# Low parts of 17 projection weights: a subtraction on VectorE replaced by a negated copy on ScalarE and an adding transfer

## The chip, the cores and the metric

The kernel runs on one core of one Trainium2 chip. The metric is the device time of one execution in microseconds; the median of three runs is compared. A core has a matrix engine (TensorE, PE in the profile, with its weight loads as PEld), three engines for elementwise work (VectorE or DVE, ScalarE or ACT, GpSimd or POOL), and SyncE (SP), which here only issues transfers. All engines run their own instruction queues in order and wait for each other through semaphores. Transfers run on 16 DMA engines beside them.

## The reference

One layer of a diffusion backbone on 512 latent tokens and 256 context tokens, width 1024, all in float32. Cut to what matters here:

```
mod = silu(c) @ w_mod + b_mod                        # shift, scale, gate
h   = rms_norm(x) * (1 + scale) + shift              # 512 + 256 tokens
cq, ckv, kr, z, xbc, dt = split(h @ w_in, [384, 256, 32, 1024, 1536, 32])
q   = rms_norm(cq) @ w_q_up ;  k, v = rms_norm(ckv) @ w_kv_up
attn = softmax(q k^T) v                              # 16 heads
ssd  = chunked bidirectional scan(silu(conv(xbc)), dt) * silu(z), normalised
x   = x + gate * rms_norm([attn, ssd] @ w_out)
x   = x + gate2 * rms_norm((gelu(conv(h2 @ w_gate)) * (h2 @ w_val)) @ w_down)
```

The columns of `w_in` for `xbc` (12 blocks of 128), `cq` (3 blocks) and `ckv` (2 blocks) are the weights in question.

## The kernel before

TensorE is used in its fast float32r format, which rounds its operands. To keep the precision, an operand `x` is split into a high part `hi = round(x)` and a low part `lo = x - hi`, both in float32r, and each product is made three times: hi·hi, hi·lo, lo·hi. `split` (line 504) does this: ScalarE copies (line 506), VectorE or, where a caller says so, GpSimd subtracts (line 507). `weight` (line 509) gets a tile, loads 128 rows of a weight through SP (`load`, line 497), gets two more tiles for the parts, and splits.

The input projection is worked in blocks of 128 output columns. `xbc(m)` (line 780, m from 0 to 11) takes one 128x1024 weight, multiplies it with the modulated tokens (`gemm_T`, line 756: 8 row blocks times 3 products, for the 512 latent tokens and, below m = 10, for the 256 context tokens), and runs the convolution on ScalarE (line 787) and VectorE (line 791). `latent` (line 822) does the same for the low-rank queries and keys/values, with sums of squares on GpSimd (line 840). Called first are xbc(10), xbc(11) and `latent("wcq")` (lines 869 to 871), then xbc(8, 0, 1, 2, 3) (line 891); the rest of the input projection (line 972) runs beside the state scan `ssd` (line 991), whose products with the decay are on GpSimd (lines 1024, 1033). Before all this TensorE works on the z projection (`half_of_z`, line 691; its product is line 693), and parts of the second half of z are spread among the later work.

The order on every engine is not that of the text. The program is traced once, then `plan` (line 389) computes a list schedule of all instructions from a table of costs, assigns buffers (53 blocks of 1024 columns, cut into 212 units), repeats this 24 times, and keeps the order with the smallest sum; in the second tracing that order is written down for every engine. So any change of an instruction or of a cost gives a new order and new buffers for the whole kernel. In that schedule a transfer is booked with an issue time (`issue`, line 200), a start latency (`DMA_START`, line 147), its bytes at 360 GB/s (`price`, line 157) and a wait (`DMA_WAIT`); for one issued by an engine other than SP (lines 357 to 360), the issuing engine was booked for 60 ns. Before the change GpSimd issues no transfer; SP issues nearly all and ScalarE a few.

Attention, the output projection (line 1318) and the MLP (line 1445 and behind) follow; they use `weight` and `split` unchanged.

Of the kernel before, what the change touches and what calls it, by code (L numbers as in the profile page):

```python
# [13 lines left out]
AF = mybir.ActivationFunctionType  # L14
ALU = mybir.AluOpType
# [131 lines left out]
DMA_START, DMA_WAIT, DMA_AHEAD, DMA_ALONE, RUN, FLYING, DMA_FULL, DMA_FILLS = 650, 910, 3000, 0.8, 80, 8, 600, 40000  # L147
# [116 lines left out]
class Graph:  # L264
# [48 lines left out]
    def schedule(self, rank, look=0.06):  # L313

        n = len(self.preds)
        left, ready = [len(p) for p in self.preds], [0.0] * n
        start, end = [0.0] * n, [0.0] * n
        later, now = {e: [] for e in ENGINES}, {e: [] for e in ENGINES}
        clock, order, queue = {e: 0.0 if self.back else BEGIN for e in ENGINES}, {e: [] for e in ENGINES}, 0.0
        ticks, held, port, flying = {}, 0, 0.0, []  # L320
        for i in range(n):
            if not left[i]:
                ready[i] = max(0.0, rank[i] - AHEAD) if i in self.opens else 0.0
                heapq.heappush(later[self.eng[i]], (ready[i], rank[i], i))

        def open_until(e, t):
            while later[e] and later[e][0][0] <= t:
                _, r, i = heapq.heappop(later[e])
                heapq.heappush(now[e], (r, i))

        for _ in range(n):
            while True:
                at = []
                for e in ENGINES:
                    open_until(e, clock[e])
                    if now[e] or later[e]:
                        at.append((clock[e] if now[e] else later[e][0][0], e))
                t, e = min(at, key=lambda v: v[0])
                open_until(e, t)
                r, i = heapq.heappop(now[e])  # L340
                sooner = [v for v in later[e] if v[1] < r and v[0] < t + (look if v[1] > r - 5000 else 0.8) * self.cost[i]]
                if not sooner:
                    break
                heapq.heappush(now[e], (r, i))
                clock[e] = min(sooner, key=lambda v: v[1])[0]
            order[e].append(i)
            if self.tables[i] not in (None, held):
                held, t = self.tables[i], t + TABLE
            if self.shared[i]:
                t = max(t, port)  # L350
                port = t + self.cost[i]
            if self.dma[i] and not self.back and len(flying) >= FLYING:
                t = max(t, flying[-FLYING])
            start[i] = t
            end[i] = t + self.cost[i] if self.back or e != "PE" else self.product(t, i, ticks)
            clock[e] = end[i] + (3 if e == "PE" else 0)
            if self.dma[i] and e != "SP":
                began = t + self.dma[i] + DMA_START + 600
                queue = max(began, queue) + self.cost[i]
                end[i], clock[e] = queue + DMA_ALONE * self.cost[i], t + 60  # L360
            if e == "SP":
                began = t + self.dma[i] + DMA_START
                queue = max(began, queue) + self.cost[i]
                end[i] = queue + DMA_ALONE * self.cost[i]
                if not self.back and t < DMA_FILLS:
                    end[i] = max(began + (1 + DMA_ALONE) * self.cost[i], queue - DMA_FULL)
                clock[e] = t + self.dma[i] if self.back else max(t + self.dma[i], queue - DMA_AHEAD)
            if self.dma[i]:
                flying.append(end[i] + DMA_WAIT)
            for j in self.succs[i]:  # L370
                ready[j] = max(ready[j], end[i] + self.wait(i, j))
                left[j] -= 1
                if not left[j]:
                    if j in self.opens:
                        ready[j] = max(ready[j], rank[j] - AHEAD)
                    heapq.heappush(later[self.eng[j]], (ready[j], rank[j], j))
        return max(end), order, start, end
# [97 lines left out]
def build(nc, tc, ctx, a, out, dbg=None, places=None):  # L475
    mm = nc.tensor.matmul
    act = nc.scalar.activation
    V, G = nc.vector, nc.gpsimd
# [10 lines left out]
    def t4(*shape, dt=F32):  # L489
        return sl.get(here(), shape or (P, 1024), dt)  # L490

    def t2(*shape, dt=F32):
        return sl.get(here(), shape or (P, 512), dt)
# [3 lines left out]
    def load(dst, src, q=None):  # L497
        (q or nc.sync).dma_start(out=dst, in_=src)
# [5 lines left out]
    def split(hi, lo, src, lo_eng=None):  # L504

        act(hi, src, AF.Copy)  # L506
        (lo_eng or V).tensor_tensor(out=lo, in0=src, in1=hi, op=ALU.subtract)  # L507

    def weight(src, width=1024, lo_eng=None):

        tw = t2 if width <= 512 else t4
        raw = tw(P, width)
        load(raw, src)
        w = tw(P, width, dt=F32R), tw(P, width, dt=F32R)
        split(*w, raw, lo_eng)
        return w

    smalls = c_([P, 512], "smalls")
# [237 lines left out]
    def gemm_T(wf, nk, cols, parts=((0, 0), (0, 1), (1, 0))):  # L756

        for k in range(nk):
            for pt in parts:
                for po, xf in cols:  # L760
                    mm(po, lhsT=wf(k, pt[0]), rhs=xf(k, pt[1]), start=(k == 0 and pt == parts[0]),  # L761
                       stop=(k == nk - 1 and pt == parts[-1]))
# [15 lines left out]
    xs, bn, bct = [None] * 2, [None] * 2, [None] * 2  # L778

    def xbc(m):  # L780
        w = weight(a["wxbc"][m])
        g = (m % 8) // 4 if m < 8 else m % 2
        pm = pget("a")
        gemm_T(blk(w), KD, both(pm) if m < 10 else ((pm[:, :S], hxv),))
        st = t4(P, T)
        for o, n in ((0, S), (S, CT))[: 2 if m < 10 else 1]:
            act(st[:, o : o + n], pm[:, o : o + n], AF.Identity, scale=cwh[:, m * 5 + 2 : m * 5 + 3], bias=cbh[:, m : m + 1])  # L787
            for j in (0, 1, 3, 4):
                d = j - 2
                lo, hi = o + max(0, -d), o + n - max(0, d)  # L790
                V.scalar_tensor_tensor(out=st[:, lo:hi], in0=pm[:, lo + d : hi + d], scalar=cwh[:, m * 5 + j : m * 5 + j + 1],  # L791
                                       in1=st[:, lo:hi], op0=ALU.mult, op1=ALU.add)
        pfree(pm)

        th = t4(P, T)
        n = T if m < 10 else S
        act(th[:, :n], st[:, :n], AF.Tanh)
        if m >= 10:
            bct[g] = t4(P, 2, S)
            V.scalar_tensor_tensor(out=bct[g][:, 1, :], in0=th[:, :S], scalar=1.0, in1=st[:, :S], op0=ALU.add, op1=ALU.mult)  # L800
            return
        V.scalar_tensor_tensor(out=st, in0=th, scalar=1.0, in1=st, op0=ALU.add, op1=ALU.mult)
        tx, tc_ = pget("b"), pget("b")
        for c in range(NKT):
            o = (c if c < NX else c - NX) * P
            nc.tensor.transpose((tx if c < NX else tc_)[:, o : o + P], st[:, c * P : (c + 1) * P], ident)
        if m < 8:
            if m % 4 == 0:
                xs[g] = [t4(P, 2, 512) for _ in range(3)]
            o = (m % 4) * P  # L810
            for i in range(3):
                src = tx[:, i * 256 : i * 256 + 256] if i < 2 else tc_[:, :256]
                act(xs[g][i][:, :, o : o + P], src.rearrange("p (c n) -> p c n", c=2), AF.Copy)
        else:
            bn[g] = t4(P, NKT, P, dt=F32R), t4(P, NKT, P, dt=F32R)
            act(bct[g][:, 0, :], st[:, :S], AF.Copy)
            for src, o, n in ((tx, 0, NX), (tc_[:, :CT], NX, 2)):
                split(bn[g][0][:, o : o + n], bn[g][1][:, o : o + n], src.rearrange("p (c n) -> p c n", c=n))
        pfree(tx, tc_)


    def latent(wn, nm, width, nrm, extra):
        rawt = []
        for m in range(nm):
            w = weight(a[wn][m])
            pm = pget("a")
            gemm_T(blk(w), KD, both(pm) if width == T else ((pm[:, :S], hxv),))
            rawt.append(t4(P, T) if width == T else t2())
            act(rawt[m], pm[:, :width], AF.Copy)
            pfree(pm)  # L830
            yield 8 if width == T else 5
# [37 lines left out]
    for m in (10, 11):  # L869
        xbc(m)  # L870
    run(latent("wcq", 3, S, "qn", SCALE))


# [5 lines left out]
    raw = t2()  # L879
# [11 lines left out]
    for m in (8, 0, 1, 2, 3):  # L891
        xbc(m)
# [834 lines left out]
```

## Time and profile before

| what | value |
|---|---|
| median of three runs | 969.3 us (968.29 to 969.58) |
| span of the profiled execution | 965.5 us |
| time of the three runs beyond that span | 2.8 to 4.1 us; the page gives no time of its own for the profiled execution |
| transfers | 137.53 MB, mean 142 GB/s, nearly all on the queue of SP |

The span runs from the first to the last instruction of the profiled execution. A row of a group names the line, the engine, the operation, the result and operands, the shape, the count, then the busy time and the mean time of one, and behind the second bar the time that the engine was idle just before these instructions, with what ended it. In a timeline the first number is the start and the second the length of a merged stretch, both in us, and in brackets stands the idle time ahead with its releaser. In a table by stretches each engine has its busy time with the count in brackets. A matrix product of 512 columns has a long record because records overlap; 24 of them in 5.68 us are some 0.24 us each.

```profile
PE   8999999999899999999999999999999999999995
PEld 8888888888787888898898887988888888887784
DVE  6999868998879998887999957953324664799998
ACT  4464327455778688788885315642323241457683
POOL 0001001756757465533201000000000056030022
PEclk9999999999999999999999999999999999999998
DMA  9943103022332341445767683241303551646874
```

These lines cut the span into 40 slices of 24.1 us; a digit is the busy share in tenths. The changed weights are loaded and used in the slices 2 to 9.

### The profile page before, as it was taken

The numbers are of one execution on the slowest core, as the hardware profiler recorded it, in microseconds if no ns is written. First come the engines' busy times: TensorE is split into PE (matmuls) and PEld (weight loads), VectorE is DVE, ScalarE is ACT, GpSimd is POOL, SyncE is SP. The second block draws the span as 40 slices with busy tenths as digits, with TensorE's granted clock in tenths as the row PEclk, the third lists the DMA queues.
The fourth block names the chain that finished last, engine by engine and source line by source line (L and its number), as shares of the span: only waits on it lengthen the run. The fifth ranks groups of instructions, "written<-read, shape, count | busy, mean of one in ns | idle before, by whom it ended". The sixth has DMA issues, their size and how long they took to land. (4 is left out here: it accounts for less than half of the span.)

```text
span 965.5 us, 14710 instructions
## 1 busy us (share of the span) xinstructions
PE 940.7 (97%) x5116; PEld 802.6 (83%) x5116; DVE 765.5 (79%) x1455; ACT 526.9 (55%) x1024; POOL 240.6 (25%) x246
## 2 busy tenths in 40 slices
PE   8999999999899999999999999999999999999995
PEld 8888888888787888898898887988888888887784
DVE  6999868998879998887999957953324664799998
ACT  4464327455778688788885315642323241457683
POOL 0001001756757465533201000000000056030022
PEclk9999999999999999999999999999999999999998
DMA  9943103022332341445767683241303551646874
GB/s 351 339 163 121 50 1 99 1 71 67 80 78 66 85 116 56 118 106 121 210 221 290 258 260 151 92 174 67 131 23 110 196 175 44 201 148 196 249 259 158
DMA packets 54586, 137.53 MB, mean 142 GB/s; under 512 B 8032, under 2 KB 11120, under 8 KB 54512
## 3 DMA queue, kind: packets, MB, share of 16 engines
q1 hardware_dynamic: 53712, 134.92, 43.7%
q10 hardware_dynamic: 800, 1.68, 0.6%
q8 instruction: 40, 0.66, 0.3%
q14 instruction: 34, 0.28, 0.1%
HBM read 114.50 MB, written 6.34 MB: 125 GB/s over the span
## 5 line engine op out<-in xcount | busy, mean ns | idle before, releaser
L761 PE MATMUL banks<-block,block 128*128 128x512 f32 (+1 forms) x2132 | 453.9, 362 | 2.2 <-ACT block L1420 1.6
L761 PEld LDWEIGHTS banks<-block,block 128*128 128x128 f32 x2132 | 359.8, 189 | 63.2 <-ACT block L1420 1.9
L506 ACT ACTIVATE block<-block 128x512 fp32r<-128x512 f32 (+4 forms) x340 | 216.5, 664 | 176.2 <-PE banks L761 39.8
L507 DVE TENSOR_TENSOR block<-block,block 128x512 fp32r<-128x512 f32 (+3 forms) x316 | 249.7, 826 | 61.7 <-ACT block L506 30.0
L1557 PE MATMUL banks<-block,block 128*128 128x512 f32 x462 | 109.5, 392 | 1.2 <-DVE block L507 0.6
L1557 PEld LDWEIGHTS banks<-block,block 128*128 128x128 f32 x462 | 86.0, 188 | 22.1 <-DVE block L507 3.6
L1195 PE MATMUL banks<-block,block 128*128 128x512 f32 (+1 forms) x384 | 92.9, 352 | 3.7 <-DMA block<-block 2.6
L507 DVE TENSOR_TENSOR block<-banks,block 128x512 fp32r<-128x512 f32 (+1 forms) x156 | 84.0, 556 | 9.2 <-ACT block L506 8.7
L1325 PE MATMUL banks<-block,block 128*128 128x512 f32 x384 | 89.4, 391 | 0.0
L506 ACT ACTIVATE block<-banks 128x256 fp32r<-128x256 f32 (+1 forms) x156 | 73.5, 494 | 21.6 <-PE banks L1211 8.0
L1325 PEld LDWEIGHTS banks<-block,block 128*128 128x128 f32 x384 | 71.5, 188 | 14.7 <-DVE block L1256 0.2
L1223 PE MATMUL banks<-block,block 128*128 128x256 f32 x384 | 71.6, 298 | 1.8 <-DVE block L1256 0.9
L1195 PEld LDWEIGHTS banks<-block,block 128*128 128x128 f32 x384 | 59.9, 189 | 11.1 <-DMA block<-block 2.5
L1199 ACT ACTIVATE block<-banks,smalls 128x768 f32<-128x768 f32 x64 | 57.7, 902 | 19.9 <-DVE smalls L1197 19.2
L1197 DVE TENSOR_REDUCE smalls<-banks 128x1 f32<-128x768 f32 x64 | 60.9, 951 | 9.5 <-PE banks L1195 7.6
L1211 PE MATMUL banks<-cst,block 128*128 128x128 f32 x384 | 66.1, 273 | 0.1
L595 DVE SCALAR_TENSOR_TENSOR block<-block,block 128x1024 f32<-128x1024 f32 x52 | 65.0, 1274 | 0.0
L1223 PEld LDWEIGHTS banks<-block,block 128*128 128x128 f32 x384 | 57.2, 189 | 6.8 <-ACT block L506 2.0
L791 DVE SCALAR_TENSOR_TENSOR block<-banks,cwh,block 128x510 f32<-128x510 f32 (+3 forms) x88 | 51.6, 622 | 12.2 <-ACT block L787 11.5
L1466 POOL TENSOR_TENSOR block<-block 128x256 f32<-128x256 f32 x11 | 10.6, 967 | 174.0 <-PE banks L761 100.5
L1211 PEld LDWEIGHTS banks<-cst,block 128*128 128x128 f32 x384 | 46.9, 140 | 8.0 <-DVE block L507 2.2
L1452 ACT ACTIVATE block<-banks,prm 128x512 f32<-128x512 f32 x22 | 17.0, 779 | 66.5 <-PE banks L761 66.5
(229 smaller groups left out, 1107.5 us busy)
## 6 DMA issues: line engine op xcount, KB each, us to landing
block<-in_wdn_dram SPq DMA_DIRECT2D x99, 256.0 KB
block<-in_wmod_dram SPq DMA_DIRECT2D x48, 512.0 KB
block<-in_wup_dram SPq DMA_DIRECT2D x44, 512.0 KB
block<-block SPq DMA_DIRECT2D x32, 256.0 KB
block<-in_wout_dram SPq DMA_DIRECT2D x16, 512.0 KB
block<-in_wxbc_dram SPq DMA_DIRECT2D x12, 512.0 KB
block<-block SPq DMA_DIRECT2D x40, 128.0 KB
block<-in_wz_dram SPq DMA_DIRECT2D x16, 256.0 KB
```

Source lines behind the costliest of these rows:

```text
L506: act(hi, src, AF.Copy)
L507: (lo_eng or V).tensor_tensor(out=lo, in0=src, in1=hi, op=ALU.subtract)
L595: V.scalar_tensor_tensor(out=junk, in0=wt, scalar=0.5, in1=vec, op0=ALU.mult, op1=ALU.mult, accum_out=acc)
L761: mm(po, lhsT=wf(k, pt[0]), rhs=xf(k, pt[1]), start=(k == 0 and pt == parts[0]), stop=(k == nk - 1 and pt == parts[-1]))
L791: V.scalar_tensor_tensor(out=st[:, lo:hi], in0=pm[:, lo + d : hi + d], scalar=cwh[:, m * 5 + j : m * 5 + j + 1], in1=st[:, lo:hi], op0=ALU ...
L1195: mm(sc[:, o : o + n], lhsT=q_[:, x_, qi * P : (qi + 1) * P], rhs=kk[:, y_, :], start=part == 0, stop=part == 2)
L1197: V.reduce_max(nm, sc[:, :T], axis=AX.X, negate=True)
L1199: act(pe, sc[:, :T], AF.Exp, bias=nm, scale=1.0, accum_out=sum_)
L1211: nc.tensor.transpose((tx if c < NX else tc_)[:, o : o + P], pe[:, s_ : s_ + P], ident)
L1223: mm(po[:, half * 256 : half * 256 + 256], lhsT=vst(c), rhs=rhs, start=(part == 0 and c == 0), stop=(part == 1 and c == NKT - 1))
L1325: mm(po[i][:, nh * 512 : nh * 512 + 512], lhsT=l[lp][:, i * P : (i + 1) * P], rhs=w[wp][:, nh * 512 : nh * 512 + 512], start=(k == 0 and l ...
L1557: mm(po[i], lhsT=l[:, lp, i * P : (i + 1) * P], rhs=w[wp], start=first and q == 0 and n == 0, stop=q == PAIRS[-1] and n == 2, skip_group_c ...
```

## The change

For the 17 weights of x/B/C and of the low-rank queries, keys and values, the low part is made in another way. ScalarE copies the raw weight to the high part as before, then copies it a second time with the scale -1 into the tile of the low part, which then holds the negated rounded weight. GpSimd issues a transfer from the raw tile to the low tile that adds what it moves to what is there, so that the low tile holds the weight less its rounded value. VectorE does nothing for these weights. The wait for the low part is a wait for that transfer. All other weights and operands are split as before. In the schedule, GpSimd is booked for 1000 ns for an issue in place of 60.

```
-                end[i], clock[e] = queue + DMA_ALONE * self.cost[i], t + 60
+                end[i], clock[e] = queue + DMA_ALONE * self.cost[i], t + (1000 if e == "Pool" else 60)
...
-    def weight(src, width=1024, lo_eng=None):
+    def weight(src, width=1024, lo_eng=None, added=False):
...
         w = tw(P, width, dt=F32R), tw(P, width, dt=F32R)
-        split(*w, raw, lo_eng)
+        if added:
+            act(w[0], raw, AF.Copy)
+            act(w[1], raw, AF.Copy, scale=-1.0)
+            G.dma_start(out=w[1], in_=raw, accum_op=ALU.add)
+        else:
+            split(*w, raw, lo_eng)
         return w
...
     def xbc(m):
-        w = weight(a["wxbc"][m])
+        w = weight(a["wxbc"][m], added=True)
...
     def latent(wn, nm, width, nrm, extra):
...
-            w = weight(a[wn][m])
+            w = weight(a[wn][m], added=True)
```

## The prediction

> **What bounds the kernel now.** I read the page's totals first, then the busy time of each engine in stretches of the span, then the groups of TensorE in the stretch where it has idle time, then the timelines of the engines around the first changed weights. In the rows below the columns after the stretch's length are the busy time (and count) of PE, of weight loads, DVE, ACT and POOL, then the granted clock, the DMA share and GB/s.
>
> ```profile
> span 965.5 us, 14710 instructions
> ...
> PE 940.7 (97%) x5116; PEld 802.6 (83%) x5116; DVE 765.5 (79%) x1455; ACT 526.9 (55%) x1024; POOL 240.6 (25%) x246
> ...
> 0.00:40.00 40.00, 37.36 (x239) 35.15 (x240) 29.57 (x75) 16.18 (x28) 0.80 (x7) 0.96 0.95 350
> 40.00:200.00 160.00, 160.00 (x851) 135.76 (x851) 141.16 (x257) 80.32 (x131) 26.90 (x23) 1.00 0.25 84
> 200.00:360.00 160.00, 153.12 (x954) 132.55 (x952) 143.09 (x268) 111.78 (x253) 103.08 (x100) 1.00 0.32 82
> 920.00:966.00 46.00, 35.29 (x156) 28.91 (x154) 40.94 (x102) 25.16 (x57) 10.53 (x6) 0.93 0.58 201
> ```
>
> TensorE is busy 940.7 of 965.5 us, so all that any edit beside it can win is 24.8 us. Of these 2.64 lie in the first 40 us and 10.7 in the last 46, where the change does nothing; 11.5 are left for the middle. The changed weights are used from about 60 us to 220 us. From 40 to 200 us TensorE has no idle time at all (160.00 of 160.00), while VectorE is busy 141.16. VectorE is thus nearly full beside an engine that is quite full: work taken from it there doesn't by itself end anything sooner. The next 160 us hold 160 - 153.12 = 6.88 us of TensorE idle. Who ended that idle time (the last columns: idle us before the group, then by releaser):
>
> ```profile
> L761 PE MATMUL banks<-block,block 128*128 128x256 f32 (+1 forms) x256 | 58.5, 351 | 0.4 <-DVE block L853 0.4
> L1195 PE MATMUL banks<-block,block 128*128 128x512 f32 (+1 forms) x146 | 37.1, 356 | 2.2 <-DMA block<-block 1.9 <-ACT block L1199 0.4
> ...
> L1223 PE MATMUL banks<-block,block 128*128 128x256 f32 x120 | 21.3, 293 | 1.6 <-DVE block L1256 0.9 <-DVE block L507 0.4 <-ACT block L506 0.3
> ...
> L1067 PE MATMUL banks<-block,block 128*128 128x512 f32 x36 | 12.0, 415 | 1.0 <-DVE smalls L537 0.9
> ...
> L1044 PE MATMUL banks<-block,sel 128*128 128x256 f32 x48 | 10.1, 294 | 0.9 <-DVE block L1052 0.9
> L806 PE MATMUL banks<-cst,block 128*128 128x128 f32 x30 | 5.0, 274 | 0.5 <-ACT block L813 0.5
> ```
>
> VectorE ended 0.4 + 0.9 + 0.4 + 0.9 + 0.9 = 3.5 us of it, ScalarE 0.4 + 0.3 + 0.5 = 1.2, transfers 1.9. The chain that ended last is no help: it is followed back only to this row, long after the last changed weight.
>
> ```profile
> 546.41 1.20 DVE block L507 x2
> ```
>
> **The change, part by part.** 17 weights change: 12 of x/B/C, 3 of the low-rank queries, 2 of keys and values, each 128x1024. From 40 to 250 us:
>
> ```profile
> L507 DVE TENSOR_TENSOR block<-block,block 128x1024 fp32r<-128x1024 f32 x17 | 21.8, 1303 | 0.4 <-issue 0.4
> ...
> L506 ACT ACTIVATE block<-block 128x1024 fp32r<-128x1024 f32 x17 | 17.7, 1055 | 15.2 <-PE banks L761 5.4 <-DMA block<-in_wxbc_dram 3.8 <-DVE block L507 3.7
> ```
>
> Removed: 17 subtractions, 21.8 us of VectorE. Worth on TensorE up to 200 us: 0, as there is no idle time to take. What the relief can reach is work of VectorE that is late after 200 us, at most the 3.5 us above; at least 0, if these waits are short dependence chains (L537 and L1052 each follow other small steps) and not backlog. Nearest rows are those five waits, and two of them (0.4 of L507 and 0.4 of L853) are plain bulk work, two are chains; I take half, 1.75 us.
>
> Added on ScalarE: a second copy with the scale -1, the same shape as the first, 17 x 1.055 = 17.9 us. It lies beside TensorE work in 40 to 200 us, where ScalarE is busy 80.32 of 160. I take 0. Without that cover, an evacuation of PSUM queued behind a copy comes 1.05 us later; for the four copies after 150 us, where TensorE begins to have idle time, that is at most 4.2 us.
>
> Added on POOL: 17 issues of a transfer, each waiting for the second copy. No row has such an issue. Bound below by an SP issue (0.33 us in the rows here), above by a whole POOL operation on 128x512:
>
> ```profile
> 77.96 38.19 SPq L498 DMA_DIRECT2D block<-in_wxbc_dram  x6
> ...
> 151.40 0.33 SPq L498 DMA_DIRECT2D block<-in_wckv_dram  x1
> ...
> 158.81 0.33 SPq L498 DMA_DIRECT2D block<-in_wckv_dram  x1
> ...
> 204.12 0.33 SPq L498 DMA_DIRECT2D block<-in_wxbc_dram  x1
> ...
> 209.04 0.33 SPq L498 DMA_DIRECT2D block<-in_wxbc_dram  x1
> ...
> 90.93 1.28 POOL L840 TENSOR_TENSOR block<-block,block 128x512 f32<-128x512 f32 x1 [1.12 <-ACT block L836]
> 92.16 0.26 POOL L936 MEMSET block<- 128x192 f32 x1
> 166.22 5.48 POOL L1024 TENSOR_TENSOR block<-block,block 128x512 f32<-128x512 f32 x4 [73.81 <-ACT block L953]
> ```
>
> 5.48 / 4 = 1.37 us; I take 1. Four weights are loaded after 150 us, 13 before 117. Up to 166 us POOL has little to do (nothing between 92.4 and 166.2), and behind the early issues only two sums of squares (L840) are queued, so the 13 hold up next to nothing. The four later ones stand in front of the products of the state scan (L1024, L1033): 4 x 1 us on an engine busy 103.08 of 160 us; taken at 0, at most 4 x 1.37 = 5.5 us.
>
> Added on the DMA engines: 17 transfers of 512 KB from SBUF to SBUF, each reading its destination too. None is in this trace. A small and a large transfer with their whole latency, and the fullest stretch:
>
> ```profile
> 559.16 2.93 DMA mod_rows<-block
> 562.15 7.49 DMA block<-mod_rows
> ...
> 48.00:52.00 4.00, 4.00 (x18) 3.06 (x17) 3.75 (x7) 3.23 (x6) 0.00 (x0) 1.00 1.02 418
> ```
>
> The first moves 1 KB, the second 512 KB. At 418 GB/s 512 KB take 1.25 us, and with a second read 2.5. So from issue to landing: at least 2.93 us, at most 7.49 + 1.25 = 8.7. I take 2.93 + 2.5 = 5.4. As load, 17 x 2.5 = 43 us spread over 160 us, of which transfers now take a quarter (0.25): no queue by that. The raw tile also comes free later, by the copy, issue and landing less the subtraction: 1.05 + 1 + 5.4 - 1.3 = 6.2 us. The loads that reuse its space can slip by as much; the six of the row at 77.96 are spread over 38.19 us with the DMA engines a quarter busy, so I take 0 for it.
> The Trainium skill ("DMA: Bandwidth & Descriptors", section "Anatomy of one DMA") gives about 2.0 us plus the bytes at 436 GB/s, 3.2 us for 512 KB by my estimate, and "Collectives: The Full Stack" (section "The bandwidth ceiling") says that a reducing transfer is slowed by its second source read, not by the add; with it the estimate is 4.4 us, and the sum would be the same.
>
> Where the new latency meets TensorE is the beginning. ScalarE's first copies, VectorE's subtractions, and the products that use them:
>
> ```profile
> 54.67 2.01 ACT L506 ACTIVATE block<-block 128x1024 fp32r<-128x1024 f32 x2
> ...
> 59.21 2.00 ACT L506 ACTIVATE block<-block 128x1024 fp32r<-128x1024 f32 x2
> ...
> 58.05 1.23 DVE L507 TENSOR_TENSOR block<-block,block 128x1024 fp32r<-128x1024 f32 x1
> ...
> 62.84 1.22 DVE L507 TENSOR_TENSOR block<-block,block 128x1024 fp32r<-128x1024 f32 x1
> ...
> 59.66 5.68 PE L761 MATMUL banks<-block,block 128*128 128x512 f32 x24
> ...
> 67.01 22.02 PE L761 MATMUL banks<-block,block 128*128 128x512 f32 x96
> ...
> L693 PE MATMUL banks<-block,block 128*128 128x512 f32 x33 | 9.1, 399 | 0.0
> ```
>
> Today the first low part is done at 59.28 and used at 59.66. Afterwards it is 54.67 + 2 x 1.055 = 56.8, plus 1 for the issue, plus 5.4: 63.2, which is 3.5 us later than the use. The second would be at about 65.3, in time for 67. The cover is the other half of the z product: L693 has 33 products between 56 and 110 us (9.1 us) that wait for none of these weights, and more behind. The planner writes the order anew with a latency for the transfer in it (lines 358 to 360 and the 0.91 us of DMA_WAIT), so I expect it to put some 16 of these ahead (16 x 5.68 / 24 = 3.8 us). Cost 0; 3.5 if they are not.
>
> **Sum** on the profiled execution: 965.5 - 1.75 + 0 = 963.75 us of span. The median shown, 969.3, is 3.8 above that span (launch and end, in no row), so the time is 963.75 + 3.8 = **967.5 us**; its own range is 965.8 (all 3.5 won) to 969.3 (nothing).
>
> **The rivals.**
> *The low parts come late (slower).* The order of every engine is fixed ahead; a transfer that takes longer than it is booked for stops TensorE in its queue, and no product behind can pass. Booked are 0.45 + 0.65 + 0.6 + 1.8 x 1.456 + 0.91 = 5.2 us from the issue to the release, by the constants in the kernel's own schedule (lines 147, 167, 204 and 358 to 360); they set the order, not the time. The point from which it decides is a latency over that. By the upper bound the excess is 8.7 - 5.2 = 3.5 us for each weight that has no slack. For: the slack of the first use today is 0.38 us, of the next few 3 to 6, and VectorE, which carries other inputs of these products, stays nearly full. Against: 96 products in a row (22 us) follow at 67, so slack grows with each weight. With two weights hit, 7 us less the 1.75 won: 969.3 + 5.25 = 974.5 us.
> The Trainium skill ("SBUF — State Buffer", section "Who interferes with whom") has a rule that would bring the same: VectorE in its two-port modes keeps GpSimd from writing descriptors. By the same section, subtractions of two tensors, the bulk here, are inferred not to do it; no run here shows either yet.
>
> *The whole backlog goes (faster).* If VectorE's lead carries through and ScalarE and the transfers of the attention inputs start earlier too, all 6.88 us of idle time in 200 to 360 vanish: 969.3 - 6.9 = 962.4 us. For: VectorE is 143.09 of 160 there. Against: ScalarE gets no relief, and 1.9 us are a transfer's.
>
> *POOL is late (slower).* The four late issues delay the state scan by up to 5.5 us, half of it seen: about 972 us. For: POOL does 103.08 of 160. Against: TensorE has projections to run beside the scan.
>
> *The relief is no relief.* VectorE waits instead of working, everything else as before: 969.3.
>
> **How the numbers follow.** Some 0.2% (1.9 us) is what a measurement of this kernel can tell from no change: below 967.4 counts as faster, above 971.2 as slower. Forecast 0.46, of it 0.22 faster and 0.24 same, as 967.5 stands on the edge. Late low parts 0.25, slower. The whole backlog 0.15, faster. Late POOL 0.07, slower. No relief 0.07, same. Faster 0.37, same 0.31, slower 0.32. The range goes from a little under the whole backlog, 962.0, to a little over two late weights, 975.0; outside remain a latency beyond every row here, or a rewritten order that gains or loses elsewhere.
>
> **What would show it.** Right: 17 fewer VectorE subtractions of 128x1024 and 17 more ScalarE copies of 1.05 us; TensorE again without idle time from 40 to 200 us; idle time in 200 to 360 us of 3.4 to 6.9 us; z products ahead of the first x/B/C weight. Late low parts: L761 idle with a transfer block<-block named as what ended it, between 57 and 90 us. Late POOL: waits for L1024 or L1033 that are longer. Wrong altogether: a TensorE idle sum after 400 us that moves by more than 2 us, since nothing of the change lies there but the new order.

## The result, and the profile after

Over 16 runs each, the changed kernel takes 971.8 us (969.3 to 974.3) and the kernel before 967.8 us (964.0 to 971.2); the ratio is 1.0047 with a 95% interval of 1.0034 to 1.0060. It is slower by about 4 us: inside the range given, but the forecast was a gain of 1.75 us. The three runs that were shown for the kernel before lay above its median of 16, and the time around the span is 2.1 us in every run of the changed kernel, not the 3.8 that the prediction took. On the median of 16 as its base, the forecast would have been 966.0; that 967.5 lies nearer to what was measured is luck.

The page after: the totals, the new DMA queue (its packets, MB and share of the span of 16 engines) and the adding transfers (median us from issue to landing at the end); then two stretches of the table by engines, of after. Columns as in the prediction.

```profile
span 968.9 us, 14787 instructions
...
PE 942.7 (97%) x5116; PEld 801.5 (83%) x5116; DVE 745.0 (77%) x1438; ACT 542.6 (56%) x1041; POOL 250.6 (26%) x263
...
q0 software_dynamic: 2448, 8.91, 4.8%
...
block<-block POOLq DMA_DIRECT2D x17, 512.0 KB, 6.3
```
```profile
40.00:200.00 160.00, 157.89 (x819) 130.67 (x818) 114.82 (x239) 93.35 (x144) 36.44 (x38) 0.99 0.51 136
200.00:360.00 160.00, 155.36 (x948) 133.29 (x947) 138.82 (x263) 112.51 (x252) 101.17 (x101) 1.00 0.34 81
```

VectorE gave up 20.5 us (765.5 to 745.0), near the 21.8 us of the removed subtractions. TensorE, which had no idle time from 40 to 200 us, now has 2.11 us there. The DMA share in this stretch doubled, from 0.25 to 0.51, and it is not spread evenly. The 44 us in which the first eleven adding transfers are issued, of before and of after:

```profile
56.00:100.00 44.00, 44.00 (x221) 36.89 (x220) 42.41 (x97) 20.94 (x31) 3.18 (x4) 1.00 0.34 111
```
```profile
56.00:100.00 44.00, 41.89 (x196) 34.52 (x194) 30.51 (x77) 30.04 (x41) 12.45 (x15) 0.96 0.99 257
```

The DMA engines go from a third full to full (in stretches as short as the ones below, the share can read a little over 1). What an adding transfer costs can be read from the page: q0 took 4.8% of the engines' span, 0.048 x 968.9 / 17 = 2.7 us of all 16 engines for each. Its issue and landing, from the view of its line:

```profile
L518 POOL DMA_DIRECT2D block<-block x17: 859/862/998, 56.0 to 231.4; - x17
...
DMA to landing us min/median/max: 4.5/6.3/13.0
...
L518 POOL DMA_DIRECT2D block<-block x11: 859/859/998, 56.0 to 99.1; - x11
```

The first two rows are of the whole span (shortest, median and longest issue in ns, first and last start), the last one of 50 to 110 us alone.

Where TensorE lost its time shows in the timelines of ScalarE, VectorE and TensorE around 80 us, of after. L516 is the plain copy, L517 the negated one. L792 (an evacuation) reads a finished sum out of PSUM, the memory in which TensorE adds up its products, and L796 on VectorE is the last reader of that PSUM bank; then the bank is free for other products.

```profile
74.97 0.63 ACT L506 ACTIVATE block<-block 128x512 fp32r<-128x512 f32 x1 [3.77 <-DMA block<-in_wkd_dram]
78.58 1.06 ACT L516 ACTIVATE block<-block 128x1024 fp32r<-128x1024 f32 x1 [2.98 <-DMA block<-in_wxbc_dram]
79.55 0.76 ACT L792 ACTIVATE block<-banks,cbh,cwh 128x512 f32<-128x512 f32 x1
```
```profile
80.34 3.10 DVE L796 SCALAR_TENSOR_TENSOR block<-banks,cwh,block 128x510 f32<-128x510 f32 x4 [1.58 <-ACT block L792]
```
```profile
67.84 13.65 PE L766 MATMUL banks<-block,block 128*128 128x512 f32 x60
83.59 12.79 PE L766 MATMUL banks<-block,block 128*128 128x512 f32 x48 [2.11 <-DVE block L796]
```

Read from the bottom: TensorE waits 2.11 us for a PSUM bank. VectorE frees the bank late because ScalarE gave it the sum late (1.58). ScalarE did so late because L792 stands in its queue behind a copy of a later weight, and that copy waited 2.98 us for the weight's load; the copy before it had waited 3.77 us for another load. So no product ever waited for an adding transfer by name. What was late were ordinary loads, on DMA engines that the adding transfers had filled, and the wait reached TensorE by way of the order on ScalarE. The load that held the copy at 78.58 was issued at 66.24 us, after the first five adding transfers (issued from 56.0 to 65.3 us, the last of them landed at 78.3), and took 12.2 us to land. A second effect lies beside this chain: an adding transfer keeps the raw tile busy, and SyncE held a later load for 2.5 us, to 71.48, until one had landed and its space was free.

The stall has a second price. The stretch with the stall and the two behind it, of after (the third number from the end is the granted clock, as a share of the full one):

```profile
80.00:84.00 4.00, 1.89 (x10) 1.49 (x9) 3.55 (x5) 4.00 (x5) 2.27 (x3) 1.00 1.03 419
84.00:88.00 4.00, 4.00 (x12) 3.09 (x11) 4.00 (x14) 3.31 (x8) 0.30 (x1) 0.57 1.07 267
88.00:92.00 4.00, 4.00 (x19) 3.29 (x18) 2.84 (x7) 2.89 (x5) 0.00 (x0) 1.00 1.06 211
```

Right after the stall the granted clock is 0.57 for 4 us and TensorE does 12 products in place of 19 or 20: some 1.7 us more. The stall and this stretch together are 3.8 us. The loss is still there later: the last product of z ends at 163.7 us after and 159.7 before. TensorE's idle time behind that moved by less: from 200 to 360 us it fell by 2.2 us, and after 400 us it rose by 1.3, under the 2 us from which the prediction would have called itself wrong altogether.

### The profile page after: what moved, and what is told of

Same layout as the page of the kernel before. It is cut to its first block, busy times and chain, and to the rows that moved or that the text cites. A ratio compares the mean times of both kernels' runs of the same rounds, so it can differ in the third digit from the quotient of the medians.

```text
span 968.9 us, 14787 instructions
## 1 busy us (share of the span) xinstructions
PE 942.7 (97%) x5116; PEld 801.5 (83%) x5116; DVE 745.0 (77%) x1438; ACT 542.6 (56%) x1041; POOL 250.6 (26%) x263
## 5 line engine op out<-in xcount | busy, mean ns | idle before, releaser
L766 PE MATMUL banks<-block,block 128*128 128x512 f32 (+1 forms) x2132 | 453.8, 362 | 3.7 <-DVE block L796 2.1
L766 PEld LDWEIGHTS banks<-block,block 128*128 128x128 f32 x2132 | 358.6, 189 | 63.6 <-ACT block L517 2.3
L506 ACT ACTIVATE block<-block 128x512 fp32r<-128x512 f32 (+5 forms) x323 | 198.3, 642 | 162.4 <-DMA block<-in_wup_dram 40.8
L507 DVE TENSOR_TENSOR block<-block,block 128x512 fp32r<-128x512 f32 (+3 forms) x299 | 226.4, 792 | 29.5 <-ACT block L506 18.7
L507 DVE TENSOR_TENSOR block<-banks,block 128x256 fp32r<-128x256 f32 (+1 forms) x156 | 83.6, 555 | 7.4 <-ACT block L506 5.0
L506 ACT ACTIVATE block<-banks 128x512 fp32r<-128x512 f32 (+1 forms) x156 | 73.8, 495 | 19.9 <-PE banks L1216 13.8
L796 DVE SCALAR_TENSOR_TENSOR block<-banks,cwh,block 128x510 f32<-128x510 f32 (+3 forms) x88 | 51.9, 621 | 19.0 <-ACT block L792 18.2
L1463 DVE TENSOR_TENSOR block<-banks,block 128x512 f32<-128x512 f32 x22 | 14.7, 686 | 54.2 <-PE banks L766 54.2
```

## The experiments

Three theories stood against each other. *Full queue*: the adding transfers take twice the DMA time that the schedule books for them, loads land late, and the chain above follows. *ScalarE*: the second copies themselves hold up the evacuation. *Order*: every edit gives a new order of the whole kernel, and this one happens to be worse. All ratios are to the kernel before, run beside it.

**The same order with cheaper transfers.** The adding is left out, so the low part holds the whole weight; the order on every engine is that of the changed kernel.

```
-            G.dma_start(out=w[1], in_=raw, accum_op=ALU.add)
+            G.dma_start(out=w[1], in_=raw)
```

> Leaves out the adding: the transfer only copies the raw weight over the low part, so the low part holds the whole weight. Order of every engine, buffers, copies and issues are those of the changed kernel; only what a transfer asks of the DMA engines differs. Full-queue theory (the adding transfers read their destination too, fill the DMA engines from 57 to 92 us, a weight load lands late, ScalarE's copy waits for it with a PSUM evacuation behind it, TensorE stalls 2.1 us near 81.5 us and then runs 3.4 us at half clock): DMA share from 57 to 92 us falls well below 1, the stall is gone, no half-clock stretch near 84 us, the time falls by 3 to 4 us to 0.999 to 1.001 of the kernel before. ScalarE theory (the second copies themselves hold up the evacuation): stall stays above 1.5 us, 1.004 to 1.005. Order theory (the new order is worse in many places): stall may go but the time stays at or above 1.003.

Measured: 1.0013 (0.9993 to 1.0032), 0.34% under the changed kernel and a little above the 0.999 to 1.001 that was expected. Of this run, the queue of the transfers, the 44 us and ScalarE's queue:

```profile
q0 software_dynamic: 2448, 8.91, 2.5%
```
```profile
56.00:100.00 44.00, 44.00 (x225) 37.21 (x225) 32.04 (x90) 31.27 (x42) 8.42 (x14) 1.00 0.73 261
```
```profile
69.68 0.63 ACT L506 ACTIVATE block<-block 128x512 fp32r<-128x512 f32 x1 [0.27 <-DMA block<-in_wkd_dram]
70.89 1.06 ACT L516 ACTIVATE block<-block 128x1024 fp32r<-128x1024 f32 x1 [0.58 <-DMA block<-in_wxbc_dram]
74.75 0.78 ACT L792 ACTIVATE block<-banks,cbh,cwh 128x512 f32<-128x512 f32 x1 [2.80 <-PE banks L766]
```

A plain transfer takes 0.025 x 964.3 / 17 = 1.4 us of the engines, half of the adding one, for the same bytes moved. The two loads are now waited for 0.27 and 0.58 us instead of 3.77 and 2.98, and L792 waits for TensorE instead of the other way round. The load that took 12.2 us to land now takes 6.3. The stall and the half clock are gone. ScalarE does the same copies in the same order, so they alone are not the cause; and the order alone isn't either. What this run doesn't separate is how much of the relief comes from emptier DMA engines and how much from raw tiles that are free sooner (4.8 us from issue to landing in the median, against 6.3); the load in question had not waited for an adding transfer. The Trainium skill ("Collectives: The Full Stack", section "The bandwidth ceiling") puts the price of a reduce-scatter in the second source read of its add, not in the add. The factor of 1.9 between the two queue shares agrees with two reads; no run here shows the read by itself.

**Book the true price.** The schedule is told that these transfers take twice the time; nothing else is changed, and a new order follows.

```
-                queue = max(began, queue) + self.cost[i]
-                end[i], clock[e] = queue + DMA_ALONE * self.cost[i], t + (1000 if e == "Pool" else 60)
+                twice = 2 if e == "Pool" else 1
+                queue = max(began, queue) + twice * self.cost[i]
+                end[i], clock[e] = queue + twice * DMA_ALONE * self.cost[i], t + (1000 if e == "Pool" else 60)
```

> The changed kernel, whose schedule books the adding transfers with twice the time on the DMA engines (2.9 in place of 1.46 us, and the landing accordingly), so the order is made anew. Full-queue theory: the schedule sees the crowding, spreads the early loads, no stall of over 1 us of TensorE between 60 and 100 us, 0.998 to 1.002. ScalarE theory: 1.003 to 1.006 as before. Order theory: anywhere from 0.997 to 1.008, with idle time elsewhere than in the changed kernel.

Measured: 0.9986 (0.9972 to 0.9999). Of this run, the 44 us, and ScalarE (line numbers are one higher):

```profile
56.00:100.00 44.00, 44.00 (x222) 37.28 (x221) 31.58 (x89) 29.68 (x42) 11.70 (x14) 1.00 0.96 237
```
```profile
76.28 0.78 ACT L793 ACTIVATE block<-banks,cbh,cwh 128x512 f32<-128x512 f32 x1 [4.17 <-PE banks L767]
```

The DMA engines are as full as in the changed kernel (0.96 against 0.99), yet TensorE has no idle time. The evacuation no longer stands behind a copy that waits for a load. This sharpens the theory: full DMA engines alone cost nothing here; what costs is an order that was made without knowing of them.

**Is it luck of the order?** One constant of the buffer assignment, 2500, is set to 2600 or 2400. No instruction changes, but order and buffers do. This was done for the kernel before, the changed kernel and the one with the doubled booking.

```
-UNITS, EDGE, MARGIN = 212, 168, 2500
+UNITS, EDGE, MARGIN = 212, 168, 2600
```

> The kernel before, with one constant of the buffer assignment moved from 2500 to 2600, which makes a new order and new buffers and changes no instruction. Order theory: the time moves by 0.3 to 0.6% either way, as much as the change did. Full-queue and ScalarE theories: within 0.2%, 0.998 to 1.002.

> The changed kernel with the same constant at 2600. Full-queue theory: DMA engines full between 57 and 92 us again and a stall of TensorE with a half-clock stretch in 60 to 100 us, 1.003 to 1.006. Order theory: anywhere from 0.997 to 1.008, and a stall in 60 to 100 us only by chance.

> The doubled booking and the constant at 2600, the order of buffers with which the changed kernel took 1.015. Full-queue theory (a schedule that knows the price keeps the loads ahead of ScalarE's copies in any order): no TensorE stall of over 1 us between 60 and 100 us, 0.997 to 1.003. Order theory (the doubled booking was a lucky order): anywhere from 0.997 to 1.015, the stall may be back.

> The changed kernel with the constant at 2400, a third order under the single booking. Full-queue theory: DMA share near 1 from 57 to 92 us again and TensorE idle time of 1 to 5 us with a half-clock stretch in 60 to 100 us, 1.003 to 1.015. Order theory: as likely without a stall there as with one, 0.997 to 1.008.

> The doubled booking with the constant at 2400, the third order under it. Full-queue theory: TensorE idle under 1 us in 56 to 100 us, 0.997 to 1.003, below all three orders under the single booking (1.0045 to 1.015). Order theory: 0.997 to 1.015.

> The kernel before with the constant at 2400, its third order. It gives the spread of orders with no change: with the first two at 1 and 0.9985, full-queue theory expects 0.997 to 1.003. Order theory expects one as bad as 1.0045 now and then.

Measured, with the idle time of TensorE from 56 to 100 us (44.00 less its busy time) in the profiled run in brackets, in us:

| kernel | constant 2500 | 2600 | 2400 |
|---|---|---|---|
| before | 1 (idle 0) | 0.9985, 0.9968 to 1.0001 (0.38) | 0.9971, 0.9956 to 0.9987 (0) |
| changed | 1.0047, 1.0034 to 1.0060 (2.11) | 1.0150, 1.0127 to 1.0174 (4.13) | 1.0045, 1.0030 to 1.0060 (1.70) |
| changed, doubled booking | 0.9986, 0.9972 to 0.9999 (0) | 0.9993, 0.9978 to 1.0008 (0.70) | 1.0005, 0.9986 to 1.0025 (0) |

The order theory has its due: without any change of an instruction the time moves by up to 0.29%. But all three orders of the changed kernel lie above all the others, and all three have an early stall of at least 1.7 us. The one at 1.015 is beyond what any theory expected (1.003 to 1.006, or up to 1.008). Of it, ScalarE, then TensorE:

```profile
79.90 1.06 ACT L517 ACTIVATE block<-block 128x1024 fp32r<-128x1024 f32 x1 [4.06 <-DMA block<-in_wxbc_dram]
...
83.99 0.58 ACT L834 ACTIVATE block<-banks 128x512 f32<-128x512 f32 x1
```
```profile
84.61 14.48 PE L766 MATMUL banks<-block,block 128*128 128x512 f32 x59 [3.22 <-ACT block L834]
```

And the one at 1.0045:

```profile
66.22 0.60 ACT L704 ACTIVATE block<-banks 128x512 f32<-128x512 f32 x1 [4.07 <-DMA gate_rows<-block]
```
```profile
72.08 4.17 PE L766 MATMUL banks<-block,block 128*128 128x512 f32 x17 [1.67 <-DVE block L652]
```

It is the same pattern each time: ScalarE waits 4 us at the head of its queue for an ordinary transfer (once a load, once the store of a row that has to leave its buffer), and what stands behind it reaches TensorE late (in the second by way of L641 and VectorE's L652, on a ScalarE without idle time from 66.2 us on). In the first of the two, the early stalls (4.13 us) and a stretch at half clock behind them explain some 6 of 14 us; the rest comes later in the span, and its cause stays open. In the second the clock stayed at 1.00, so the early stall explains 1.7 of some 4 us there.

**Which transfers.** First the twelve later weights alone (the edit shown), then the first five alone (x/B/C blocks 10 and 11 and the three of the queries; `m >= 10` and `width == S`).

```
-        w = weight(a["wxbc"][m], added=True)
+        w = weight(a["wxbc"][m], added=m < 10)
...
-            w = weight(a[wn][m], added=True)
+            w = weight(a[wn][m], added=width == T)
```

> The first five weights (x/B/C blocks 10 and 11, the three of the queries) are split by subtraction on VectorE as before, the other twelve by the adding transfer, single booking. Full-queue theory: five fewer transfers of some 2.7 us between 56 and 68 us, so the loads behind them land earlier; stall of TensorE in 60 to 100 us under 1 us, 0.998 to 1.002. If the later six transfers before 100 us are enough to crowd it: 1.003 to 1.006. Order theory: 0.997 to 1.008 with no relation to the DMA share.

> Only the first five weights by the adding transfer, the other twelve by subtraction, single booking. Full-queue theory: DMA share near 1 only from 57 to about 75 us; whether ScalarE's copies of the next loads stall TensorE decides, 0.999 to 1.005. Relief of VectorE is five subtractions alone, so nothing is gained after 200 us. Order theory: 0.997 to 1.008.

Measured: 0.9997 (0.9981 to 1.0012) for the twelve, 1.0014 (0.9993 to 1.0036) for the five. The idle time of the twelve from 56 to 100 us (1.23 us, where under 1 was expected) was ended by VectorE's small steps, not by an evacuation. The five alone do give a stall of the known kind, of this run:

```profile
74.89 6.52 PE L766 MATMUL banks<-block,block 128*128 128x512 f32 x28 [1.39 <-DVE block L796]
```

There the granted clock stayed at 1.00, and the total isn't clear of no change. A second stall of that run, 1.71 us just before 100 us, was ended by GpSimd's sums of squares (L845) and is of another kind. So the first five are enough for the stall, the later twelve without them cost nothing that can be measured, and a stall of 1 to 3 us can be lost in what a new order gives or takes.

**Relief without price.** The transfer is left out (low part = negated rounded weight), both copies remain.

```
-            G.dma_start(out=w[1], in_=raw, accum_op=ALU.add)
```

> Leaves out the adding transfer: the low part stays the negated rounded weight, both ScalarE copies remain, VectorE has no subtraction and the DMA engines no added work; a new order. It is the whole relief of VectorE without its price. If the relief were worth what the forecast took (half to all of 3.5 us): 0.996 to 0.998. If TensorE's full stretch hides it: 0.998 to 1.002. ScalarE theory: a stall of over 1 us in 60 to 100 us remains, 1.003 or more. Full-queue theory: no stall there.

Measured: 0.9995 (0.9979 to 1.0010). Only its times are used, no profile, so whether an early stall remains isn't seen. VectorE is relieved of its 17 subtractions, the DMA engines have no added work, and the time is that of before: the relief is worth nothing that can be told from a new order. The ScalarE theory, which asked for 1.003 or more, falls here a second time.

**The subtraction on GpSimd.** No transfer, no second copy.

```
-        w = weight(a["wxbc"][m], added=True)
+        w = weight(a["wxbc"][m], lo_eng=G)
...
-            w = weight(a[wn][m], added=True)
+            w = weight(a[wn][m], lo_eng=G)
```

> The 17 low parts by a subtraction on GpSimd, no transfer and no second copy, in its own order: VectorE is relieved, the DMA engines are left alone. Full-queue theory: no crowding, DMA share from 57 to 92 us as before the change; 0.998 to 1.003, unless the subtractions, about twice as long there as on VectorE, come late: then TensorE waits for them by name and 1.002 to 1.008.

Measured: 1.0074 (1.0053 to 1.0095). The DMA share from 56 to 100 us is 0.29, so nothing is crowded. Of this run, GpSimd's subtractions from 50 to 215 us, then VectorE while the first five run:

```profile
L507 POOL TENSOR_TENSOR block<-block,block 128x1024 fp32r<-128x1024 f32 x15 | 40.4, 2705 | 64.3 <-ACT block L506 31.8 <-PE banks L766 21.6 <-issue 6.8
```
```profile
55.15 0.69 DVE L624 TENSOR_TENSOR block<-block,block 128x512 f32<-128x512 f32 x1
...
56.35 2.80 DVE L624 TENSOR_TENSOR block<-block,block 128x512 f32<-128x512 f32 x1
...
61.39 2.84 DVE L624 TENSOR_TENSOR block<-block,block 128x512 f32<-128x512 f32 x1
64.16 2.30 DVE L647 SCALAR_TENSOR_TENSOR scx<-modc,prm 128x1 f32<-128x1 f32 x1
```

The miss is in how: TensorE didn't wait for the subtractions but 4.17 us for L624, whose additions took 2.8 us instead of 0.69 while GpSimd worked, and an operation on a single column (L647) 2.3 us. The Trainium skill ("SBUF — State Buffer", section "Who interferes with whom") says that a VectorE instruction with two SBUF inputs contends with a GpSimd instruction that reads SBUF, under an exclusive lock on a port that the two share. These rows agree.

The fastest kernel of all is the one before with the constant at 2400, 0.9971: a better order of the same work, which has nothing to do with the change.

## Why the prediction was wrong

- **Removed subtractions, "I take half, 1.75 us"**: not borne out. The removal happened, but the relief without its price measured 0.9995, with an interval (0.9979 to 1.0010) that just reaches the 0.9982 of 1.75 us. Idle time from 200 to 360 us did fall, from 6.88 to 4.64 us, and not on VectorE's account: of after, the largest row there is still VectorE's.

```profile
L1049 PE MATMUL banks<-block,sel 128*128 128x256 f32 x48 | 10.1, 299 | 3.0 <-DVE block L1057 2.9
```

  With the smaller rows of VectorE (0.7 and 0.2) that is 3.8 us, against 3.5 before. So the waits that the prediction halved did not get shorter; the measured end of its own bounds is the lower one, 0. They are not only short chains, as it gave for that bound: ahead of the longest one (1.4 us) VectorE worked without idle time from 261.0 to 262.8 us, two convolution steps (L796) among the scan's own.
- **ScalarE's copies at 0**: right as an amount (1.05 us each, and the same copies cost nothing in the same order with cheaper transfers). They did form the queue in which a late load becomes a late evacuation.
- **POOL's issue at 1 us, cost 0**: right as an amount, 0.86 us; TensorE waited for none of the state scan's GpSimd products by name (L1029 and L1038 in the changed kernel).
- **The transfer's latency, 5.4 us**: median 6.3, up to 13.0 against the bound of 8.7. The load on the engines was sized well: 2.5 us forecast, 2.7 measured.
- **"As load, 17 x 2.5 = 43 us spread over 160 us ... no queue by that"**: this is the step that failed, and with it the next one, that loads may slip at no cost. The average came out as the sum has it (0.25 + 43 / 160 = 0.52; measured 0.51), but it is no measure of a queue. Eleven of the 17 transfers are issued within 44 us, where 11 x 2.7 = 30 us of them meet the loads of the next weights, and the DMA share is 0.99; the five issued before 66 us were enough for the stall. The prediction took the six loads of the row at 77.96 as spread over its 38.19 us. That row is a merged stretch: four of the six are issued by 82 us, and of before, without any adding transfer, the DMA engines are already full there for a while.

```profile
80.00:84.00 4.00, 4.00 (x19) 3.30 (x18) 4.00 (x10) 2.12 (x3) 0.00 (x0) 1.00 0.98 359
```
- **The rival of late low parts** had the sign, the place (57 to 90 us, L766) and a fitting trigger, a price above the one booked. It is also what made the range wide enough to hold the measured time. Its path was another: the excess hit the loads behind the transfers, then ScalarE's queue, then a PSUM bank. Its test, a transfer named as what ended L766's idle time, would have said no. It also left out the half clock that followed, nearly half of the 3.8 us.
- **The new order**: three orders of the kernel before differ by up to 0.29%, more than the 1.75 us that the forecast rested on. A gain of that size, had it come, could not have been told from what a new order gives or takes.

## What to carry to other kernels

Work moved to transfers is paid in DMA time at the place where it happens: sum it over the stretch in which the transfers are issued, with the loads that share it, and not over the whole stage. An adding transfer took 1.9 times the DMA time of a plain one here, and where a schedule is computed from costs, the true cost of a new operation has to be in it; here the doubled booking alone turned 1.0047 into 0.9986, 1.0150 into 0.9993 and 1.0045 into 1.0005. And before relief of a busy engine is counted as a gain, look whether the engine that sets the end has any idle time there: TensorE had none.

## What the hardware showed beside

- An adding transfer of 512 KB from SBUF to SBUF took 2.7 us of all 16 DMA engines, a plain one 1.4 us. From issue to landing the 17 adding ones took 4.5 to 13.0 us.
- A TensorE stall of 2.11 us was followed by 4 us at a mean granted clock of 0.57, one of 3.22 us (the run at 1.015) by 4 us at 0.65. After stalls of 1.67 and 1.39 us in other runs the clock stayed at 1.00. The Trainium skill ("TensorE: Matmul & The Clock Gate", section "Why this matters for your kernels") warns of gaps of over about 3 us; here a shorter one was enough once.
- A VectorE addition of 128x512 went from 0.69 to 2.8 us beside GpSimd's subtractions.
